# Split-operand query-key products in the stick-breaking group of a hybrid mixer trunk

## The chip, the cores and the metric

The kernel runs on one core of a Trainium2 chip. The metric is the device time of one execution in microseconds (us). The kernel before took 978.83 us, the median of three runs (978.14 to 978.84).

## The reference

One transformer block on x [512, 1024], fp32. Four mixers read the normed input: a causal pooling mixer, a dilated attention (12 heads of 64), a stick-breaking attention (4 heads of 128) and a diagonal state-space mixer (S5). Their outputs are gated, projected, summed and projected once more; then comes a gated feed-forward layer (FFN). The part that is changed is the first product of the stick-breaking group:

```python
xn = rmsnorm(x, attn_norm_g)
proj = xn @ w_in                      # 1024 -> 4864
y_sb = stick_breaking_attention(qkv_sb)
#   per block of 128 queries:
#   z = einsum('bhqe,bhke->bhqk', qb, kh) / sqrt(128)
#   w = where(mask, exp(log_sigmoid(z) + excl_cumsum(log_sigmoid(-z))), 0)
#   o = w @ vh
for yb, width in zip((y_pool, y_dil, y_sb, y_s5), BRANCH_WIDTHS):
    merged += sigmoid(xn @ w_gate[b]) * (yb @ w_branch[rows])
x = x + merged @ w_out                # "x2" in the kernel
x = x + (silu(hn @ w_up_g) * (hn @ w_up_u)) @ w_down   # hn = rmsnorm(x2)
```

## The kernel before

Every big product is done in three passes. A weight chunk is fetched by DMA (`raw`), ScalarE casts it to the rounded type fp32r (`hi`), VectorE subtracts (`lo = raw - hi`). The activations are split in the same way, and `mm3` adds hi·hi, hi·lo and lo·hi into one PSUM bank. `split(src, nm)` is the same for one 128x512 tile: a ScalarE copy into `<nm>h`, a VectorE subtraction into `<nm>l`, both in new slots. The few products that are left in plain fp32 go to TensorE as one instruction each; one of them shows in the profile as several records.

The order of the instructions on each engine is written by the Python program: the scheduler does not change it. The main stream goes through the weight chunks: the S5 input (u5), the dilated group's q, k and v (`qk`, `v`), then `sb_qk(0)`, `sb_v(0)`, `pool_u(0)`, `pool_u(1)`, `sb_qk(1)`, `sb_v(1)`, then the gates and branch projections of branch 0 (pool), 1 (dilated), 2 (stick-breaking), 3 (S5), the output projection `m_o`, and the FFN. Beside it run generators (`s5_gen`, `dil_gen`, `sb_gen`, `pool_gen`). The function `tick()`, called after most products of the main stream, lets each of them emit its next piece. It holds them back when the program's own count of time (`clock`, fed by the wrapper `_Paced`, which charges a plain fp32 product four times its columns) says that VectorE or ScalarE is more than MAX_LAG behind TensorE. So an edit of a cost or a count of instructions can move where later pieces stand in the queues. Every instruction that goes through `_Paced` is recorded with line 81, so instructions are told apart by the names of their tiles.

VectorE and ScalarE carry out their queues strictly in the written order: an instruction that waits holds up all behind it.

All 128x512 working tiles come out of one rotating pool, `slots`, of N_SLOTS buffers. When a new tile gets a buffer that another tile had, its first writer waits until the last reader of that other tile is done.

Names used below: `m_sqk` and `sqk` are a stick-breaking q or k product and its evacuation (`sb_qk`), `m_sv` the v product (`sb_v`), `s_z` the query-key product (`sb_gen`). `s_pw`, `yph`, `ypl` are the pooling mixer's group product and its split output; `p`, `ph`, `pl` its split input (`pool_gen`). `prob`, `s_pt`, `wt`, `s_po`, `ydil` are the dilated group's probabilities, their transposes on TensorE, these in SBUF, the product with v, and the sum. `pw_c`, `s_re`, `s_im`, `s_psy`, `h_re`, `h_im`, `ta`, `tb` belong to S5, where `s_psy` is a TensorE group that reads `pw_c` and `s_re`. `m_g` and `m_b` are the gate and branch products.

Of the kernel before, what the change touches and what calls it, by code (L numbers as in the profile page):

```python
# [43 lines left out]
CST_CNT = 512  # L44
CST_W = CST_CNT + 64

N_SLOTS = 61
N_RAW = 2
N_PM = 3
S5_RATE = 0.9  # L50
# [35 lines left out]
def _advance(clock, key, cost):  # L86
    clock[key] = cost + (clock[key] if key == "pe" else max(clock[key], clock["pe"]))
# [3 lines left out]
def hybrid_trunk(ctx: ExitStack, tc: tile.TileContext, a: dict, out: bass.AP):  # L91
# [5 lines left out]
    PE = _Paced(nc.tensor, lambda n: _advance(clock, "pe", max(0.42e-3 * n, 0.1)))  # L97
    ctx.enter_context(tc.manual_schedule())

    gp = ctx.enter_context(tc.tile_pool(name="consts", bufs=1))  # L100
    sp = ctx.enter_context(tc.tile_pool(name="slots", bufs=N_SLOTS))
    wp = ctx.enter_context(tc.tile_pool(name="weights", bufs=2))
# [10 lines left out]
    def nm_(nm):  # L113
        uid[0] += 1
        return f"{nm}_{uid[0]}"

    def slot(nm):
        return sp.tile([P, T], F32, tag="s", name=nm_(nm))
# [5 lines left out]
    def main_ps(nm):  # L124
        return pm.tile([P, T], F32, tag="mm", name=nm_("m_" + nm))

    def side_ps(nm):
        return pa.tile([P, T], F32, tag="at", name=nm_("s_" + nm))

    def r_(t):  # L130
        return t.bitcast(F32R)

    def split(src, nm, mk=None):
        mk = mk or slot
        hi = mk(nm + "h")
        lo = mk(nm + "l")
        A.copy(r_(hi), src)
        V.tensor_tensor(r_(lo), src, hi, ALU.subtract)
        return r_(hi), r_(lo)
# [124 lines left out]
    def next_chunk():  # L264
        c = used[0]
        used[0] += 1
        while len(loaded) < min(len(ready) + N_RAW, len(specs)):
            load_next()
        while len(ready) < min(c + 2, len(specs)):
            if specs[len(ready)][0] == "w_ups":  # L270
                flush(split_steps())
            else:
                split_next()
        return ready[c]

    def mm3(ps, ch, c, nw, acts, k0=0):
        n = len(acts)
        for k, (ah, al) in enumerate(acts):
            wh, wl = ch.h(k0 + k, c, P, nw), ch.l(k0 + k, c, P, nw)
            PE.matmul(ps, wh, ah, start=k == 0, stop=False)  # L280
            PE.matmul(ps, wh, al, start=False, stop=False)
            PE.matmul(ps, wl, ah, start=False, stop=k == n - 1)
# [8 lines left out]
    def tick(force=False):  # L291
        for e in list(active):
            e[3] += e[2]
            if e[3] < 1.0 and not force:
                continue
            e[3] -= 1.0
            if e[1] > 0:
                e[1] -= 1
                continue
            if max(clock["v"], clock["a"]) - clock["pe"] > MAX_LAG and not force:  # L300
                continue
            try:
                w = next(e[0])
                e[1] = (w or 1) - 1
            except StopIteration:
                active.remove(e)
# [10 lines left out]
    ps = side_ps("warm")  # L317
# [6 lines left out]
    for kt in range(KT):  # L324
        t = slot("x")
# [32 lines left out]
    def g2(kt):  # L358
        return cols[:, 8 + kt : 9 + kt]
# [5 lines left out]
    def sumsq_add(acc, src):  # L365
        sq = slot("sq")
        A.activation(sq, src, AF.Square)
        if acc is None:
            return sq
        V.tensor_tensor(acc, acc, sq, ALU.add)  # L370
        return acc
# [561 lines left out]
    sq, sk, sv = [], [], []  # L933
# [5 lines left out]
    def sb_gen():  # L939
        units = [(h, b) for h in range(4) for b in range(4)]  # L940
        bes, wts, pos = {}, {}, {}
        for s in range(len(units) + SB_T + SB_O):
            if s >= SB_T + SB_O:
                u = s - SB_T - SB_O
                h, b = units[u]
                if b == 0:
                    pos[h] = side_ps("sbo")
                for c in range(b + 1):
                    PE.matmul(
                        pos[h][:, b * P : (b + 1) * P],  # L950
                        sv[h // 2][c // 2][:, (c % 2) * 256 + (h % 2) * P : (c % 2) * 256 + (h % 2) * P + P],
                        wts[u][:, c * P : (c + 1) * P],
                        start=c == 0,
                        stop=c == b,
                    )
                if b == 3:
                    ysb.append(split(pos[h], "sb"))
            if SB_T <= s < len(units) + SB_T:
                u = s - SB_T
                h, b = units[u]  # L960
                n = (b + 1) * P
                pt = side_ps("wt")
                for c in range(b + 1):
                    PE.transpose(pt[:, c * P : (c + 1) * P], bes[u][:, c * P : (c + 1) * P], ident)
                wts[u] = slot("wt")
                A.copy(wts[u][:, :n], pt[:, :n])
            if s < len(units):
                h, b = units[s]
                n = (b + 1) * P
                dg = slice(b * P, n)  # L970
                ps = side_ps("z")
                PE.matmul(ps[:, :n], sq[h][:, dg], sk[h][:, :n], start=True, stop=True)
                be, om = slot("be"), slot("om")
                bes[s] = be
                A.activation(om[:, :n], ps[:, :n], AF.Sigmoid, scale=-z_scale)
                A.activation(be[:, :n], ps[:, :n], AF.Sigmoid, scale=z_scale)
                V.tensor_tensor(om[:, dg], om[:, dg], m_up, ALU.max)
                V.tensor_tensor(be[:, dg], be[:, dg], m_low, ALU.mult)
                V.tensor_tensor_scan(om[:, :n][:, ::-1], om[:, :n][:, ::-1], zcol.to_broadcast([P, n]), 1.0, ALU.mult, ALU.add)
                V.tensor_tensor(be[:, : n - 1], be[:, : n - 1], om[:, 1:n], ALU.mult)  # L980
            yield
# [88 lines left out]
    for g in range(3):  # L1070
        for lst, scale in ((dq, rb8), (dk, rb)):
            ch = next_chunk()
            for n in range(2):
                ps = main_ps("qk")
                mm3(ps, ch, n * P, 256, xg)
                t = slot("qk")
# [4 lines left out]
        if g == 0:  # L1081
            vt = [slot("v"), slot("v")]
            for b in range(4):
                ps = main_ps("v")
# [10 lines left out]
        else:  # L1095
            for n in range(2):
                ps = main_ps("v")
                mm3(ps, ch, n * P, 256, xg)
                t = slot("vf")
# [6 lines left out]
    def sb_qk(c):  # L1106
        for lst in (sq, sk):
            ch = next_chunk()
            for n in range(2):
                ps = main_ps("sqk")  # L1110
                mm3(ps, ch, n * P, 256, xg)
                t = slot("sqk")
                V.tensor_tensor(t, ps, rb, ALU.mult)
                lst.append(t)
                tick()

    def sb_v(c):
# [14 lines left out]
    def pool_u(c):  # L1132
        ch = next_chunk()
        for n in range(2):
# [5 lines left out]
            tick()  # L1140

    sb_qk(0)
    sb_v(0)
    pool_u(0)
    pool_u(1)
    sb_qk(1)
    sb_v(1)
    e_sb = start(sb_gen(), SB_RATE)


# [33 lines left out]
    for c in range(2):  # L1184
        ch = next_chunk()
        for n in range(2):
# [4 lines left out]
            t = slot("sg")  # L1191
# [4 lines left out]
    for kt in range(KT):  # L1196
        t = slot("xo")
# [8 lines left out]
    def keep(nm):  # L1206
        n = nm_(nm)
        return fp.tile([P, T], F32, tag=n, name=n)
# [3 lines left out]
    x2, x2g = [], []  # L1212
    acc = None
    for c in range(4):
        ch = next_chunk()
        for n in range(2):
            nt = 2 * c + n
            ps = main_ps("o")
            mm3(ps, ch, n * P, 256, mg)
            t = keep("x2")  # L1220
            V.tensor_tensor(t, ps, xo[nt], ALU.add)
            x2.append(t)
            hi, lo = slot("x2h"), slot("x2l")
            A.activation(r_(hi), t, AF.Copy, scale=g2(nt))
            V.scalar_tensor_tensor(r_(lo), t, g2(nt), hi, ALU.mult, ALU.subtract)
            x2g.append((r_(hi), r_(lo)))
            acc = sumsq_add(acc, t)
# [115 lines left out]
    for part in range(2):  # L1343
# [33 lines left out]
        for nt in range(8 - N_HALVED * part):  # L1377
# [8 lines left out]
            ps = main_ps("d")  # L1386
# [22 lines left out]
    def down_add(nt, hf, ps):  # L1409
        sl = slice(H * hf, H * hf + H)  # L1410
        V.tensor_tensor(x2[nt][:, sl], ps[:, 0:H], x2[nt][:, sl], ALU.add)
        sq = slot("sq")
        A.activation(sq[:, sl], x2[nt][:, sl], AF.Square)
        return sq
# [25 lines left out]
    for nt, ch in last:  # L1440
        ps = main_ps("d")
        down_half(nt, ch, 0, ps, kall)
        t = down_add(nt, 0, ps)
        V.tensor_tensor(acc[:, 0:H], acc[:, 0:H], t[:, 0:H], ALU.add)
    for nt, ch in last[:-1]:
        ps = main_ps("d")
        down_half(nt, ch, 1, ps, kall)
        t = down_add(nt, 1, ps)
# [5 lines left out]
    ps = main_ps("d")  # L1454
# [5 lines left out]
    t = down_add(nt, 1, ps)  # L1460
# [140 lines left out]
```

## Time and profile before

| | |
|---|---|
| median of 3 runs | 978.83 us (978.14 to 978.84) |
| the profiled execution | 980.17 us |
| its span | 978.4 us |
| TensorE busy | 963.7 us, 99% |
| VectorE busy | 656.8 us, 67% |
| ScalarE busy | 409.1 us, 42% |
| TensorE on the chain that ended last | 96% |

PE is TensorE, DVE is VectorE, ACT is ScalarE. Busy time is the time in which the engine had an instruction in work. The chain is followed back from the last instruction of the program: at each step to what released it, or to the instruction before it on the same engine. In the timelines, "[0.54 <-ACT hi L81]" behind an instruction says that its engine stood idle for 0.54 us before it, and what ended that. Matmuls overlap: one record of 0.39 us does not mean that the next started 0.39 us later, so costs are taken from the distance between starts.

### The profile page before, as it was taken

To read this page: it belongs to the slowest core of one execution; us is meant where nothing else is said; L and a number is where in the kernel's file an instruction comes from. 1 tells how busy PE (TensorE), PEld (TensorE's weight loads), DVE (VectorE), ACT (ScalarE), POOL (GpSimd) and SP (SyncE) were. 2 spreads that over 40 slices of the span, in tenths; PEclk is the share of its full clock that TensorE was granted. 3 is DMA by queue.
4 is the path that set the end of the run, shared out by engine and by line. 5 is a ranking of instruction groups with operands and counts; after the bars stand their busy time and mean duration, and the time that the engine had idled before them with its cause. 6 is when DMAs were issued, how large, how long until landed. Compare 5 with 4: busy or idle time off the path is not lost.

```text
span 978.4 us, 13757 instructions
## 1 busy us (share of the span) xinstructions
PE 963.7 (99%) x5426; PEld 831.3 (85%) x5426; DVE 656.8 (67%) x1253; ACT 409.1 (42%) x712; POOL 4.3 (0%) x20
## 2 busy tenths in 40 slices
PE   8999999999999999999999999999999999999996
PEld 6887888988888888887888888888898899999886
DVE  6576667588777976955645555488973379997344
ACT  7343533343446334227433343345442235554231
POOL 1000000000000000000000000000000000000000
PEclk9999999999999999999999999999999999999998
DMA  7442232231113113262342332313223323232212
GB/s 276 167 127 97 61 118 89 68 111 45 66 55 102 55 43 119 92 203 87 120 169 89 109 119 91 124 52 122 83 71 110 102 92 125 87 130 75 103 60 86
DMA packets 38696, 100.26 MB, mean 102 GB/s; under 512 B 14222, under 2 KB 22075, under 8 KB 32872
## 3 DMA queue, kind: packets, MB, share of 16 engines
q1 hardware_dynamic: 38632, 99.38, 30.2%
q8 instruction: 43, 0.70, 0.3%
q14 instruction: 21, 0.17, 0.1%
HBM read 94.94 MB, written 4.42 MB: 102 GB/s over the span
## 4 chain that ended last, share of the span: by engine, by line
PE 96%; DVE 2%; ACT 1%; DMA 1%; issue 0%; SPq 0%; DVEq 0%
PE m_g L81 17%; PE m_d L81 12%; PE s_fa L81 9%; PE m_b L81 7%; PE m_qk L81 7%; PE m_fb L81 6%; PE m_sqk L81 4%; PE m_o L81 4%; PE m_fg L81 4%; PE m_v L81 3%; PE m_u L81 3%; PE m_fu L81 3%; PE m_sv L81 2%; PE s_u L81 1%; PE s_fu L81 1%; PE m_gb L81 1%
## 5 line engine op out<-in xcount | busy, mean ns | idle before, releaser
L81 DVE TENSOR_TENSOR lo<-raw,hi 128x1024 fp32r<-128x1024 f32 (+5 forms) x207 | 197.8, 988 | 52.4 <-ACT hi L81 51.5
L81 ACT CAST hi<-raw 128x1024 fp32r<-128x1024 f32 (+5 forms) x207 | 169.3, 861 | 68.8 <-PE m_d L81 30.0
L81 PE MATMUL m_g<-xh,hi 128*128 128x512 f32 x256 | 102.7, 401 | 0.0
L81 PE MATMUL m_g<-xh,lo 128*128 128x512 f32 x256 | 100.0, 391 | 0.3 <-DVE lo L81 0.3
L81 PE MATMUL m_g<-xl,hi 128*128 128x512 f32 x256 | 99.7, 389 | 0.0
L81 PE MATMUL m_d<-hh,hi 128*128 128x512 f32 (+1 forms) x198 | 72.5, 366 | 0.0
L81 PE MATMUL m_d<-hl,hi 128*128 128x512 f32 (+1 forms) x198 | 72.4, 366 | 0.0
L81 PE MATMUL m_d<-hh,lo 128*128 128x512 f32 (+1 forms) x198 | 72.3, 365 | 0.0
L81 ACT ACTIVATE gt<-gt 128x512 f32<-128x512 f32 x32 | 20.2, 632 | 109.7 <-DVE gt L81 109.7
L81 PEld LDWEIGHTS m_g<-xh,lo 128*128 128x128 f32 x256 | 48.1, 188 | 11.2 <-DVE lo L81 1.0
L81 PEld LDWEIGHTS m_g<-xh,hi 128*128 128x128 f32 x256 | 48.1, 188 | 10.9 <-issue 1.0
L81 PEld LDWEIGHTS m_g<-xl,hi 128*128 128x128 f32 x256 | 48.1, 188 | 10.8 <-issue 1.0
L81 DVE TENSOR_TENSOR x<-m_d,x 128x512 f32<-128x512 f32 (+1 forms) x18 | 11.4, 632 | 62.6 <-PE m_d L81 62.6
L81 PEld LDWEIGHTS m_d<-hh,lo 128*128 128x128 f32 x198 | 37.3, 189 | 6.1
L81 PEld LDWEIGHTS m_d<-hh,hi 128*128 128x128 f32 x198 | 37.4, 189 | 6.0
L81 PEld LDWEIGHTS m_d<-hl,hi 128*128 128x128 f32 x198 | 37.4, 189 | 5.9
L81 DVE TENSOR_TENSOR gt<-m_b,gt 128x512 f32<-128x512 f32 x24 | 16.5, 689 | 38.0 <-PE m_b L81 32.8
L81 ACT ACTIVATE prob<-prob,nmx 128x128 f32<-128x128 f32 (+1 forms) x48 | 20.1, 419 | 49.3 <-DVE nmx L81 49.2
L81 DVE TENSOR_TENSOR raw<-raw 128x512 f32<-128x512 f32 (+1 forms) x45 | 39.1, 870 | 1.6
L81 PE MATMUL m_qk<-xh,hi 128*128 128x512 f32 x96 | 38.2, 397 | 0.0
L81 PE MATMUL m_qk<-xl,hi 128*128 128x512 f32 x96 | 37.4, 390 | 0.0
L81 PE MATMUL m_qk<-xh,lo 128*128 128x512 f32 x96 | 37.4, 390 | 0.0
(400 smaller groups left out, 2498.0 us busy)
## 6 DMA issues: line engine op xcount, KB each, us to landing
raw<-in_w_g SPq DMA_DIRECT2D x24, 768.0 KB, 4.3
raw<-in_w_in SPq DMA_DIRECT2D x17, 1024.0 KB, 6.9
raw<-in_w_ups SPq DMA_DIRECT2D x15, 1024.0 KB, 4.8
raw<-in_w_down SPq DMA_DIRECT2D x16, 704.0 KB, 4.0
raw<-in_w_up SPq DMA_DIRECT2D x7, 1024.0 KB, 4.8
raw<-in_w_g SPq DMA_DIRECT2D x8, 640.0 KB, 3.8
raw<-in_w_out SPq DMA_DIRECT2D x4, 1024.0 KB, 4.9
x<-in_x SPq DMA_DIRECT2D x8, 256.0 KB, 4.9
```

What stands on the lines that cost most here:

```text
L81: return f(out, *args, **kw)
```

## The change

The evacuated q and k tiles of the stick-breaking group are split into a rounded and a rest part. The query-key product becomes three fp32r passes on these parts where it was one plain fp32 product. The eight x2 tiles, which had buffers of their own in the FFN's pool, come from the rotating pool, and that pool has 67 buffers where it had 61.

```diff
-N_SLOTS = 61
+N_SLOTS = 67
...
-                PE.matmul(ps[:, :n], sq[h][:, dg], sk[h][:, :n], start=True, stop=True)
+                (qh, ql), (kh, kl) = sq[h], sk[h]
+                PE.matmul(ps[:, :n], qh[:, dg], kh[:, :n], start=True, stop=False)
+                PE.matmul(ps[:, :n], qh[:, dg], kl[:, :n], start=False, stop=False)
+                PE.matmul(ps[:, :n], ql[:, dg], kh[:, :n], start=False, stop=True)
...
                 V.tensor_tensor(t, ps, rb, ALU.mult)
-                lst.append(t)
+                lst.append(split(t, "sqk"))
...
-            t = keep("x2")
+            t = slot("x2")
```

There are 16 query-key products, four heads with 128, 256, 384 and 512 columns each, and eight q and k tiles, so eight new casts `sqkh` on ScalarE and eight new subtractions `sqkl` on VectorE. In the written order the change has effects in three places.

TensorE, the first query-key product, at the start of branch 0. The kernel before:

```order
L81 MATMUL s_po_2619<-wt_2471,v_654 64x128
L81 MATMUL s_po_2619<-wt_2559,v_654 64x128
L81 MATMUL s_pt_2636<-cst,prob_1254 128x128 [waits DVE_49] x4
L81 MATMUL s_z_2647<-sqk_1614,sqk_1519 128x128
L81 MATMUL m_b_2657<-yph_2176,hi_2383 128x512
L81 MATMUL m_b_2657<-ypl_2177,hi_2383 128x512
```

The changed kernel:

```order
L81 MATMUL s_pt_2623<-cst,prob_1019 128x128
L81 MATMUL s_z_2634<-sqkh_1624,sqkh_1521 128x128
L81 MATMUL s_z_2634<-sqkl_1625,sqkh_1521 128x128
L81 MATMUL s_z_2634<-sqkh_1624,sqkl_1522 128x128
L81 MATMUL m_b_2646<-yph_2100,hi_2383 128x512
L81 MATMUL m_b_2646<-ypl_2101,hi_2383 128x512
```

The place of the product in the stream is the same; three instructions stand where one stood, and other units of the dilated group are beside it.

VectorE, during `sb_qk(0)`, from the second q/k tile to the S5 operand `pw_c`. The kernel before:

```order
L81 TENSOR_SCALAR nmx<-stat_207 128x4
L81 TENSOR_TENSOR sqk_1558<-m_sqk_1533,rb 128x512
L81 TENSOR_TENSOR h_re_1354<-h_re_1354,sin_1073 128x512
L81 TENSOR_TENSOR h_im_1355<-h_im_1355,cos_1074 128x512
L81 TENSOR_TENSOR s_im<-h_re_1354,h_im_1355 128x4x127
L81 TENSOR_TENSOR lo_1584<-raw_1486,hi_1583 128x1024 x2
L81 TENSOR_TENSOR sqk_1614<-m_sqk_1589,rb 128x512
L81 TENSOR_TENSOR t_251_1616<-s5p,pwr_712 128x256
L81 TENSOR_TENSOR t_251_1616<-s5p,pwi_713 128x256
```

The changed kernel:

```order
L81 TENSOR_SCALAR nmx<-stat_207 128x4
L81 TENSOR_TENSOR sqk_1562<-m_sqk_1537,rb 128x512
L81 TENSOR_TENSOR sqkl_1565<-sqk_1562,sqkh_1564 128x512
L81 TENSOR_TENSOR h_re_1354<-h_re_1354,sin_1073 128x512
L81 TENSOR_TENSOR h_im_1355<-h_im_1355,cos_1074 128x512
L81 TENSOR_TENSOR s_im<-h_re_1354,h_im_1355 128x4x127
L81 TENSOR_TENSOR lo_1592<-raw_1486,hi_1591 128x1024 x2
L81 TENSOR_TENSOR sqk_1622<-m_sqk_1597,rb 128x512
L81 TENSOR_TENSOR sqkl_1625<-sqk_1622,sqkh_1624 128x512
L81 TENSOR_TENSOR t_257_1628<-s5p,pwr_712 128x256
L81 TENSOR_TENSOR t_257_1628<-s5p,pwi_713 128x256
```

Each subtraction stands directly behind the evacuation whose ScalarE copy it needs, and ahead of S5's instructions.

VectorE, at the end of `sb_qk(1)`, ahead of the v product `m_sv`; here with the engines that an instruction waits for. The kernel before:

```order
L81 TENSOR_TENSOR ydil_2159<-s_po_2304,ydil_2159 128x512 [waits PE_49]
L81 TENSOR_SCALAR prob_1366<-prob_1366,fp_1919 128x128 x4
L81 SCALAR_TENSOR_TENSOR ypl_2330<-s_pw_2325,cols,yph_2329 128x512 [waits Activation_49]
L81 TENSOR_TENSOR sqk_2358<-m_sqk_2333,rb 128x512 [waits PE_49]
L81 TENSOR_TENSOR h_re_2296<-h_re_2296,ta_2298 128x512 [waits DVE_49]
```

The changed kernel:

```order
L81 SCALAR_TENSOR_TENSOR ypl_2329<-s_pw_2324,cols,yph_2328 128x512 [waits PE_49,Activation_49]
L81 SCALAR_TENSOR_TENSOR p_2332<-s_356_2253,u_2077 128x496 [waits PE_49]
L81 TENSOR_TENSOR s_356_2253<-s_356_2253,cst 128x16
L81 TENSOR_TENSOR p_2332<-s_356_2253,u_2077 128x16 [waits DVE_49]
L81 TENSOR_TENSOR pl_2337<-p_2332,ph_2336 128x512 [waits PE_49,Activation_49]
L81 TENSOR_TENSOR sqk_2365<-m_sqk_2340,rb 128x512 [waits PE_49]
L81 TENSOR_TENSOR sqkl_2368<-sqk_2365,sqkh_2367 128x512 [waits Activation_49]
```

And on TensorE, what follows the first half of the v product in the changed kernel:

```order
L81 MATMUL m_sv_2417<-lo_2259,xh_174 128x256
L81 MATMUL s_po_2446<-wt_2236,v_1211 64x128 [waits PE_49]
L81 MATMUL s_po_2446<-wt_2318,v_1211 64x128 [waits Activation_49]
L81 MATMUL s_po_2446<-wt_2236,v_1211 64x128
```

One pooling unit (`p`, `pl`) has moved back behind `ypl`, and `ypl_2329` has a wait on TensorE that its counterpart `ypl_2330` did not have. The buffer that `ypl_2329` is given belonged to `wt_2236`, whose last readers are the `s_po_2446` products behind the 48 matmuls of `m_sv`.

## Rows read from the trace of the kernel before

**Rows 1.** The page, part 1: busy us, share, instructions, by engine.

```profile
PE 963.7 (99%) x5426; PEld 831.3 (85%) x5426; DVE 656.8 (67%) x1253; ACT 409.1 (42%) x712; POOL 4.3 (0%) x20
```

**Rows 2.** TensorE's waits: us in total, times, longest.

```profile
PE s_u L81 <- ACT hi L81: 2.9, 2, 1.5
```

**Rows 3.** TensorE's timeline in the FFN: start us, us, what, idle before.

```profile
697.87 0.39 PE L81 MATMUL s_fa<-xsh,hi 128*128 128x256 f32 x1 [1.62 <-ACT mu L81]
```

**Rows 4.** A window: us, busy (instructions) by engine, clock, DMA share, GB/s.

```profile
150.00:255.00 105.00, 105.00 (x660) 91.67 (x659) 78.46 (x188) 39.65 (x74) 0.00 (x0) 1.00 0.26 80
```

**Rows 5.** The chain, 165 to 290 us: start us, us, what.

```profile
173.03 11.51 PE m_sv L81 x96
...
239.12 0.44 PE s_pt L81 x4
...
262.90 0.22 PE s_z L81 x2
...
269.42 5.46 PE m_g L81 x24
...
276.60 0.65 PE s_z L81 x2
...
280.64 0.86 PE s_z L81 x2
```

**Rows 6.** VectorE's timeline in sb_qk(1), sb_v(1): start, us, what, idle before.

```profile
225.37 0.67 DVE L81 SCALAR_TENSOR_TENSOR p<-s,u 128x496 f32<-128x496 f32 x1
...
227.03 0.69 DVE L81 TENSOR_TENSOR pl<-p,ph 128x512 fp32r<-128x512 f32 x1 [0.69 <-ACT ph L81]
...
236.88 0.74 DVE L81 SCALAR_TENSOR_TENSOR ypl<-s_pw,cols,yph 128x512 fp32r<-128x512 f32 x1
...
239.76 0.68 DVE L81 TENSOR_TENSOR h_re<-h_re,ta 128x512 f32<-128x512 f32 x1
...
243.50 1.06 DVE L81 TENSOR_SCALAR prob<-prob,f 128x128 f32<-128x128 f32 x4
244.47 1.82 DVE L81 TENSOR_TENSOR lo<-raw,hi 128x768 fp32r<-128x768 f32 x2
...
248.14 0.68 DVE L81 TENSOR_TENSOR ydil<-s_po,ydil 128x512 f32<-128x512 f32 x1
```

**Rows 7.** VectorE's timeline in sb_qk(0).

```profile
154.50 0.68 DVE L81 TENSOR_TENSOR sqk<-m_sqk,rb 128x512 f32<-128x512 f32 x1
155.10 0.68 DVE L81 TENSOR_TENSOR ta<-h_re,cos 128x512 f32<-128x512 f32 x1
...
158.62 0.69 DVE L81 TENSOR_TENSOR sqk<-m_sqk,rb 128x512 f32<-128x512 f32 x1 [0.47 <-PE m_sqk L81]
...
161.77 2.36 DVE L81 TENSOR_TENSOR lo<-raw,hi 128x1024 fp32r<-128x1024 f32 x2 [0.54 <-ACT hi L81]
...
167.66 0.42 DVE L81 TENSOR_TENSOR pw_c<-t 64x256 f32<-64x256 f32 x1
```

**Rows 8.** ScalarE's timeline, same stretch.

```profile
158.19 0.40 ACT L81 ACTIVATE prob<-prob,nmx 128x128 f32<-128x128 f32 x1 [5.04 <-DVE nmx L81]
```

**Rows 9.** TensorE's timeline, same stretch.

```profile
170.41 0.39 PE L81 MATMUL s_psy<-s_re,pw_c 128*128 128x128 f32 x2
```

**Rows 10.** The chain of waits, 230 to 250 us.

```profile
232.97 0.70 PE s_pw L81 x3
...
239.55 5.74 PE m_sv L81 x48
245.29 1.02 PE s_po L81 x16
```

**Rows 11.** Windows as in rows 4, about three waits of TensorE.

```profile
8.00:12.00 4.00, 2.79 (x9) 1.94 (x9) 3.07 (x5) 3.87 (x6) 0.00 (x0) 0.84 1.06 405
12.00:16.00 4.00, 4.00 (x15) 3.19 (x14) 3.76 (x6) 3.94 (x7) 0.00 (x0) 0.73 1.11 387
...
698.00:702.00 4.00, 4.00 (x34) 4.00 (x35) 3.90 (x5) 1.89 (x4) 0.00 (x0) 1.00 0.73 262
```

## The prediction

> **What bounds the kernel now.** I read the engines' busy times first, then TensorE's waits, then one window around the change, then the chain and the timelines inside it. TensorE is busy for 963.7 of 978.4 us, VectorE for 67% and ScalarE for 42% [rows 1]. Its waits for other engines are few: the two largest entries are 2.9 us in two waits near the start [rows 2] and 1.62 us in one at 697.87 us, in the FFN [rows 3]. So nearly every microsecond of TensorE's queue counts, and the rest counts only where it makes TensorE wait. Between 150 and 255 us, where q, k, v and the pooling input of the changed group are made, TensorE does not idle at all, and VectorE works for 78.46 of 105 us [rows 4]: 75%, above its mean. All new VectorE work falls there. The question is whether the remaining 25% lies where it is wanted.
>
> **The query-key products.** On the chain the products of 128, 384 and 512 columns take 0.22, 0.65 and 0.86 us [rows 5]; in proportion the one of 256 takes 0.43. Four heads make 4 x 2.16 = 8.64 us. Each becomes three fp32r passes. The gate product has 24 such passes of 512 columns in 5.46 us, 0.2275 each; the v product has 96 of 256 columns in 11.51 us, 0.12 each [rows 5]. The line through both is 0.0125 us plus 0.42 ns a column, which gives 0.066 for 128 and 0.174 for 384 columns. After: 4 x 3 x (0.066 + 0.12 + 0.174 + 0.2275) = 7.05 us, a gain of 1.6. No row shows a 128-column pass in fp32r. At best the fixed part is nothing: the passes go by 0.42 ns a column, 1280 columns x 12 x 0.42 = 6.45 us, a gain of 2.2. At worst such a pass is as long as the whole plain product of that size, 0.22: then 12 passes take 2.64 instead of 0.79 and the edit costs 0.26. I take 1.6, by the line through the two nearest sizes; a plain 128-column transposition is 0.11 (four in 0.44 [rows 5]), and with that number the gain is 1.06.
>
> The passes of 256 columns, each with a load of other weights, follow one another after 0.12 us [rows 5]. The Trainium skill, "TensorE: Matmul & The Clock Gate", section "LDWEIGHTS (loading the stationary operand)", says that a load takes its columns divided by 1.2 in nanoseconds, 107 ns for 128. By that rule a 128-column pass would be bound by its load, at 0.107 instead of 0.066 us, and the sum would be higher by an estimated 0.5 us. No run here shows such a pass; 0.12 lies above both, so the row does not decide.
>
> **The splits in sb_qk(0).** A subtraction stands directly behind its evacuation, so VectorE waits for ScalarE's cast between the two. The nearest pair of that form is `ph` and `pl`: 0.69 us idle, then the subtraction [rows 6], which occupies 0.60 (the distance between the starts of neighbouring 512-column operations, 154.50 to 155.10 [rows 7]). So 1.3 to 1.4 us each; I use 1.37 with the hand-over. Eight make 11 us of VectorE's queue, and the price is what its idle time does not absorb. Behind the first (evacuated at 154.50) comes `nmx`, and the second evacuation had 0.47 us of idle ahead of it [rows 7]: it starts 0.9 late, at 159.5. Its cast is worse off, since it queues behind four exponentials on ScalarE, which began at 158.19 [rows 8] and now begin as late as `nmx` does; the subtraction cannot start before about 161.7, and S5's `h_re` behind it is 3.1 us late. The 0.54 of idle before `lo` [rows 7] gives back some: `lo` is 2.5 late, the next evacuation 1.7, and with its own subtraction `pw_c` is 3.06 late. The third `pw_c` ended at 168.08 (167.66 + 0.42 [rows 7]); its first reader, an `s_psy` product, started at 170.41 [rows 9]: 2.33 us of slack. So TensorE waits 0.7 us there. Bounds: nothing, if the casts slip in before the exponentials, and 2.2, if the second cast waits behind the two v copies as well.
>
> **The freed buffer in sb_qk(1).** Live at once are now eight more tiles (parts of q and k) with six more buffers, so buffers come round later. In the order, `ypl_2329` on VectorE waits for a TensorE reader of its buffer's last tenant, `wt_2236`; this reader stands behind the 48 matmuls of `m_sv`. Before, `ypl` ran at 236.88, ahead of `m_sv` at 239.55 [rows 6, 10]. VectorE's queue is strict, so from there to the end of the following `s_po` it does nothing. Call the start of `m_sv` A. `m_sv` takes 5.74 and `s_po` 1.02 [rows 10]: `ypl` starts at A+6.78. Queued behind it are a pooling unit's `p`, its cast and `pl`. `p` starts one `ypl` later, at A+7.43; from `p` to `pl` it took 1.66 (225.37 to 227.03 [rows 6]), so the cast ends and `pl` starts at A+9.09, and `pl` ends at A+9.78. TensorE goes on from `s_po` through `s_pt` (0.44 [rows 5]) and one `s_pw` group (0.70 [rows 10]) and stands at A+7.9 before the second `s_pw` group. Its first pass wants the cast and waits 1.2; the second pass, 0.23 later, wants `pl` and waits 0.5. Together **1.7 us**.
>
> TensorE then does the other half of `m_sv` and is at A+16.0 before `s_pt`, which reads a `prob` of VectorE's. VectorE, from A+9.78, has the fourth `sqk` of this stage with its split (0.60 + 0.69 + 0.60), `h_re` to the end of the scans (239.76 to 243.50, 3.74), `lo` to `ydil` (244.47 to 248.14, 3.67 [rows 6]), `ydil` itself (0.60) and the first `prob` (0.28): A+20.0. Before, `sqk` was already done when `m_sv` began, and none of this stood in arrears. So TensorE waits another **4.0 us**. Bounds of the two waits together: nothing, if VectorE gets to `ypl` only when the buffer is free anyway or the queue behind it has slack that I don't see; 7.5, if the casts on ScalarE are late by as much as in sb_qk(0). I take 5.7, as the chain of rows gives it. After these two VectorE has the room of branch 0 to catch up; the later query-key products keep their places.
>
> **The clock.** A wait of TensorE can cost more than itself. Near the start it waited 2.9 us [rows 2] and the granted clock was 0.84 from 8 to 12 and 0.73 from 12 to 16 us [rows 11]: taken as a mixture of the two levels, 1.2 and 2.4 GHz, this is 1.3 and 2.2 us at 1.2 GHz, which lost 1.7 us of work. Behind the single wait of 1.62 us at 697.87 it stayed at 1.00 [rows 3, 11]. A wait of 4.0 us that follows one of 1.7 by 6 us is more like the first. I charge one fall, 1.6 us; bounds: none, and two falls, 3.4.
>
> **The rest.** Eight more casts on ScalarE, 0.62 each, are hidden where they don't appear above: it is busy 42% of the time. x2 in the rotating pool moves nothing in the FFN's order; 67 - 8 = 59 buffers serve there where 61 did. The trace cannot show a reuse that gets tight; I price it at nothing, because every instruction keeps its place, and one wait, if it came, at about the 1.62 us of the one that the FFN has [rows 3].
>
> **The sum.** -1.6 + 0.7 + 1.7 + 4.0 + 1.6 = +6.4. The profiled execution took 980.17 us (span 978.4, and 1.8 around it), which makes 986.6; it was 1.3 over the median, 978.83, so the runs should give **985.2**.
>
> **Rivals.** *A: the splits are absorbed, the products alone count.* For it: VectorE has 25% free, and a TensorE wait on a buffer costs nothing if the buffer is free by then. Against it: the place of the reader, behind `m_sv`, while VectorE reached `ypl` 2.7 us before `m_sv` began. The point from which it decides is whether VectorE comes to `ypl` later than A+6.78. Then 978.83 - 1.6 = 977.2, or 976.6 with no fixed part: the other side, about at the limit of what can be told. *B: the waits come, the clock holds*, as at 697.87: 983.6. *C: one of the two waits in sb_qk(1) is absorbed*: 978.83 - 1.6 + 0.7 + 1.7 or 4.0, and no fall: 979.6 to 981.9. *D: the short passes are slow* (0.22 each, nothing else changed): 1.85 more, 987.1. *E: the clock falls more than once and the `s_psy` wait is 2.2*: 985.2 + 1.5 + 1.7 = 988.4.
>
> **Chances.** Forecast 0.38, B 0.26, A 0.14 (half of it below the limit), C 0.10, D 0.05, E 0.07. A measurement of this kernel can tell about 0.2% from no change: 976.87 to 980.79. Faster 0.07; the same 0.11 (the other half of A and not quite half of C); slower 0.82. The range 979.5 to 988.6 leaves out A and a little above; the forecast's own is 984 to 987.
>
> **What would show it.** The products: three `s_z` records where one set stood, 0.2, 0.36, 0.52 and 0.68 us on the chain. The splits: a wait of TensorE for VectorE before `s_psy` near 170 us. The buffer: VectorE idle for some 6 us before a `ypl`, released by `s_po`; then TensorE waiting for `ph`/`pl` before `s_pw`, and for `prob` before `s_pt`. The clock: a granted clock under 1 after that wait. It is wrong if no such idle time stands before `ypl`, if TensorE's waits grow elsewhere (in the FFN, at x2), or if `s_z` takes more than before.

## The result

The changed kernel takes 986.40 us (median of four runs, 986.08 to 988.25), the kernel before 978.84 on the same chip: a ratio of 1.0079, interval 1.0062 to 1.0097, or 7.6 us more. The forecast was 985.2.

The profile after, part 1 of its page: busy time, share of the span (984.2 us) and count of instructions.

```profile
PE 964.4 (98%) x5442; PEld 833.2 (85%) x5442; DVE 662.1 (67%) x1261; ACT 413.2 (42%) x720; POOL 4.3 (0%) x20
```

TensorE works as long as before [rows 1], and the span is 5.8 us longer. The sums over the whole program tell little; the list of TensorE's waits tells more (in total, times, longest):

```profile
PE s_pt L81 <- DVE prob L81: 3.5, 1, 3.5
PE s_u L81 <- ACT hi L81: 2.5, 2, 2.1
PE s_fa L81 <- ACT mu L81: 1.6, 1, 1.6
...
PE s_pw L81 <- ACT ph L81: 1.2, 1, 1.2
...
PE s_psy L81 <- DVE pw_c L81: 0.6, 1, 0.6
...
PE s_pw L81 <- DVE pl L81: 0.2, 1, 0.2
```

`s_u` and `s_fa` were there before [rows 2, 3]. The four others are new: `s_psy` in sb_qk(0), two before `s_pw` and one before `s_pt` around sb_v(1), 5.5 us together. The reason for the last three stands in VectorE's timeline there, which answers to [rows 6]:

```profile
237.23 0.87 DVE L81 TENSOR_SCALAR prob<-prob,fp 128x128 f32<-128x128 f32 x4
243.65 0.75 DVE L81 SCALAR_TENSOR_TENSOR ypl<-s_pw,cols,yph 128x512 fp32r<-128x512 f32 x1 [5.55 <-PE s_po L81]
244.32 0.67 DVE L81 SCALAR_TENSOR_TENSOR p<-s,u 128x496 f32<-128x496 f32 x1
...
246.02 0.69 DVE L81 TENSOR_TENSOR pl<-p,ph 128x512 fp32r<-128x512 f32 x1 [0.74 <-ACT ph L81]
246.63 0.68 DVE L81 TENSOR_TENSOR sqk<-m_sqk,rb 128x512 f32<-128x512 f32 x1
248.00 0.69 DVE L81 TENSOR_TENSOR sqkl<-sqk,sqkh 128x512 fp32r<-128x512 f32 x1 [0.69 <-ACT sqkh L81]
...
256.60 0.87 DVE L81 TENSOR_SCALAR prob<-prob,fp 128x128 f32<-128x128 f32 x4
```

VectorE stands idle for 5.55 us, released by `s_po`, before an instruction that ran without a wait before. From there to 256.60 its queue is one unbroken line of work but for two short casts, and at its end stands the `prob` that TensorE wants.

The pieces of the chain that answer to [rows 5] (start us, us, what):

```profile
169.48 2.84 PE s_psy L81 x22
...
256.93 1.10 PE s_pt L81 x4
258.03 6.70 PE m_g L81 x24
...
266.67 0.28 PE s_z L81 x3
266.95 2.82 PE m_b L81 x12
269.78 2.68 PE s_psy L81 x24
...
273.22 0.35 PE s_z L81 x3
273.57 5.45 PE m_g L81 x24
...
281.40 0.52 PE s_z L81 x3
...
285.33 0.70 PE s_z L81 x3
```

The products cost 0.28, 0.35, 0.52 and 0.70 us, 7.4 for all, where they cost 8.64. A little of that comes back in the twelve branch passes directly behind a product of 128 columns. Before, the first such group was shorter:

```profile
263.12 2.75 PE m_b L81 x12
```

In all four heads the branch passes at this place take 2.82, 2.82, 2.78 and 2.78 us in the changed kernel, 11.20 together, where they took 11.01; the gain is 1.2 on the products alone and 1.0 with these.

The first 24 gate passes after the long wait take 6.70 us, the next 24 take 5.45. The clock accounts for it, in windows as in [rows 11] (clock: the eighth column, behind POOL's busy time):

```profile
8.00:12.00 4.00, 2.87 (x11) 2.06 (x12) 3.15 (x5) 3.94 (x7) 0.00 (x0) 1.00 1.04 392
12.00:16.00 4.00, 4.00 (x20) 3.28 (x19) 3.68 (x6) 3.97 (x7) 0.00 (x0) 1.00 1.06 380
254.00:258.00 4.00, 1.07 (x5) 0.99 (x6) 3.97 (x10) 0.84 (x2) 0.00 (x0) 0.89 0.61 197
258.00:262.00 4.00, 4.00 (x14) 3.15 (x13) 3.96 (x10) 3.33 (x4) 0.00 (x0) 0.69 0.00 0
```

After the wait of 3.55 us part of the time runs at 1.2 GHz. At the start it is the other way round: this execution has 1.00 there where the profiled one of before had 0.84 and 0.73, which lost it 1.7 us. So 5.8 + 1.7 = 7.5 us are to be explained between the two traces, which agrees with the 7.6 of the medians.

### The profile page after: what moved, and what is told of

Same layout as the page of the kernel before. It is cut to its first block, busy times and chain, and to the rows that moved or that the text cites. A ratio compares the mean times of both kernels' runs of the same rounds, so it can differ in the third digit from the quotient of the medians.

```text
span 984.2 us, 13807 instructions
## 1 busy us (share of the span) xinstructions
PE 964.4 (98%) x5442; PEld 833.2 (85%) x5442; DVE 662.1 (67%) x1261; ACT 413.2 (42%) x720; POOL 4.3 (0%) x20
## 4 chain that ended last, share of the span: by engine, by line
PE 91%; DVE 5%; ACT 2%; issue 1%; DMA 1%; SPq 0%; DVEq 0%; ACTq 0%
PE m_g L81 17%; PE m_d L81 12%; PE s_fa L81 9%; PE m_b L81 7%; PE m_qk L81 7%; PE m_fb L81 6%; PE m_o L81 4%; PE m_fg L81 4%; PE m_u L81 3%; PE m_fu L81 3%; PE m_v L81 2%; PE m_sqk L81 2%; PE m_sv L81 2%; DVE lo L81 1%; PE s_fu L81 1%; PE m_gb L81 1%
```

## The experiments

**One buffer more.** 68 buffers instead of 67.

```diff
-N_SLOTS = 67
+N_SLOTS = 68
```

> The changed kernel with 68 buffers in place of 67. In VectorE's queue this frees only the one ypl of its wait for TensorE; the p directly behind it still gets a buffer whose last reader stands behind m_sv. Theory (VectorE's strict queue is held by a buffer that TensorE frees only after m_sv): VectorE still idles, now before p; the first wait (s_pw for ph) shrinks by one ypl, 0.65 us, the later one of 3.5 us for prob stays: about 985.7, 0.7 less than the changed kernel. Rival 1 (the pool is short by a single buffer): both waits go and the time is about 979. Rival 2 (the waits come from the added work on VectorE, buffers don't matter): 986.4, no change.

Measured: 985.69 us, 1.0068 of the kernel before (1.0056 to 1.0081). TensorE's waits, and VectorE's timeline at the place:

```profile
PE s_pt L81 <- DVE prob L81: 3.6, 1, 3.6
...
PE s_pw L81 <- ACT ph L81: 0.5, 1, 0.5
```

```profile
239.87 0.75 DVE L81 SCALAR_TENSOR_TENSOR ypl<-s_pw,cols,yph 128x512 fp32r<-128x512 f32 x1
...
245.46 0.68 DVE L81 SCALAR_TENSOR_TENSOR p<-s,u 128x496 f32<-128x496 f32 x1 [4.84 <-PE s_po L81]
```

`ypl` runs at once, and the next instruction takes its place as the one that is held: 4.84 us of idle in place of 5.55, the same releaser. The first wait shrank by 0.7 us, the later one stayed, as the theory had it. The time alone does not decide: the loss is 6.2 us over the kernel before timed beside it (979.54), where it was 7.6, and the two intervals overlap. The rows decide against rivals 1 and 2. A window behind the waits shows the clock, the figure behind POOL's:

```profile
255.00:300.00 45.00, 41.91 (x275) 35.13 (x276) 36.43 (x89) 19.09 (x41) 0.00 (x0) 0.96 0.21 65
```

**The low parts unread.** The same instructions on VectorE and ScalarE in the same order up to branch 0, but eight tiles come free at once.

```diff
-                PE.matmul(ps[:, :n], qh[:, dg], kh[:, :n], start=True, stop=False)
-                PE.matmul(ps[:, :n], qh[:, dg], kl[:, :n], start=False, stop=False)
-                PE.matmul(ps[:, :n], ql[:, dg], kh[:, :n], start=False, stop=True)
+                PE.matmul(ps[:, :n], qh.bitcast(F32)[:, dg], kh.bitcast(F32)[:, :n], start=True, stop=True)
```

> The changed kernel, but the query-key product is one plain fp32 product of the two rounded parts; the rest parts are computed and never read, so the products lack their low bits. VectorE and ScalarE do the same instructions in the same order up to branch 0; what differs is that the eight unread rest parts give their buffers back at once, and ypl and p lose their wait for TensorE. Theory (buffers): no wait of TensorE near 245 to 257 us, the one of 0.6 before s_psy stays with some 0.4 of restart; the products cost 8.64 as before: about 979.8. Rival (the added VectorE and ScalarE work itself makes the waits): 986.4 + 1.2 for the plain products = 987.6.

Measured: 980.78 us against 979.54 of the kernel before timed beside it, 1.0017 (1.0008 to 1.0027). VectorE's timeline:

```profile
239.70 0.86 DVE L81 TENSOR_SCALAR prob<-prob,fp 128x128 f32<-128x128 f32 x4
240.48 0.74 DVE L81 SCALAR_TENSOR_TENSOR ypl<-s_pw,cols,yph 128x512 fp32r<-128x512 f32 x1
241.14 0.66 DVE L81 SCALAR_TENSOR_TENSOR p<-s,u 128x496 f32<-128x496 f32 x1
...
253.42 0.86 DVE L81 TENSOR_SCALAR prob<-prob,fp 128x128 f32<-128x128 f32 x4
```

VectorE no longer idles before `ypl`, and the second group of `prob` starts 13.7 us after the first (253.42 - 239.70), where it takes 19.4 in the changed kernel (256.60 - 237.23). Among TensorE's waits past the start and ahead of the FFN one of some size is left:

```profile
PE s_psy L81 <- DVE pw_c L81: 0.5, 1, 0.5
```

This is the run that shows the cause: all of the added VectorE and ScalarE work is still there, and the loss falls from 7.6 us to 1.2, although the products are back at their old price. What made the three waits was how long eight tiles hold their buffers.

**x2 alone.** The kernel before with the second part of the change.

```diff
-N_SLOTS = 61
+N_SLOTS = 67
...
-            t = keep("x2")
+            t = slot("x2")
```

> The kernel before with only the second part of the change: x2 in the rotating pool and 67 buffers. The order on every engine is that of before. Theory: 978.8, the same within 0.5. Rival (x2's place costs a wait in the FFN, or more buffers help the kernel before): more than 1 us to either side.

Measured: 980.15 us against 979.54, 1.0006 (0.9998 to 1.0015): not to be told from no change. Its list of waits has the entries of before and no other.

**The subtraction after tick().** With 68 buffers.

```diff
-                lst.append(split(t, "sqk"))
-                tick()
+                hi, lo = slot("sqkh"), slot("sqkl")
+                A.copy(r_(hi), t)
+                tick()
+                V.tensor_tensor(r_(lo), t, hi, ALU.subtract)
+                lst.append((r_(hi), r_(lo)))
```

> The changed kernel with 68 buffers, and the subtraction of each q and k split emitted after tick() in place of directly behind the evacuation, so that other VectorE work stands between it and ScalarE's cast. This also moves the dilated and pooling units back to earlier ticks, and the ypl ahead of m_sv has no wait for TensorE. Theory: all three waits go and the products' gain of 1.2 is left: about 977.6. Rival (the added work makes the waits wherever it stands): 983 or more.

> The same kernel as subtract_after_tick, on the chip of this group, as the base of the five-fold products and to see its sign: 1.0 below the kernel before by its trace from the first v product to the end of the query-key products, 0.2 below by its first timing.

Measured: 979.29 us against 979.54, 0.9995 (0.9986 to 1.0004), and again 978.30 against 978.95, 0.9995 (0.9987 to 1.0004). The window of [rows 4], in the first of the two:

```profile
150.00:255.00 105.00, 105.00 (x658) 91.49 (x657) 80.46 (x189) 43.41 (x82) 0.00 (x0) 1.00 0.26 80
```

TensorE does not idle, and VectorE works for 80.46 us in it, more than before. So the added work does fit, at this order and with 68 buffers. The time is not above that of the kernel before, but the gain of 1.2 that was expected isn't shown either: the two medians lie 0.25 and 0.65 us lower, inside their intervals. It is the best version found, and no faster than the kernel before as far as can be told.

**Only the last subtraction late.** 67 buffers; the edit of the run above for the last q/k tile only.

```diff
+                if c == 1 and lst is sk and n >= 1:
...
+                else:
                     lst.append(split(t, "sqk"))
                     tick()
```

> The changed kernel with 67 buffers; only the last of the eight subtractions is emitted after tick(), the others stay directly behind their evacuations. The ypl keeps its buffer wait behind m_sv, but the VectorE queue behind it is shorter by one wait for ScalarE, and units of the dilated and pooling groups move. Theory (the chain of VectorE work behind the held ypl sets the later wait): TensorE's wait for prob falls from 3.5 to about 1.4 us. If the clock holds behind such a wait, as behind the 1.62 us in the FFN, the time is 978.8 - 1.2 + 1.0 (s_psy) + 1.4 + 0.3 (restart) + 0.7 (a new wait of the stick-breaking transposes for ScalarE) = 981.0; if it falls as behind the 3.5 us, 982.9. Rival (the last subtraction isn't on the path): 986.4.

Measured: 981.43 us, 1.0029 (1.0018 to 1.0040). TensorE's wait and the window behind it:

```profile
PE s_pt L81 <- DVE prob L81: 1.3, 1, 1.3
```

```profile
250.00:254.00 4.00, 4.00 (x36) 4.00 (x35) 3.97 (x8) 1.18 (x4) 0.00 (x0) 1.00 0.23 43
```

The time and the wait came close to what the theory gave, but two premises of the expectation were wrong. The new wait of 0.7 us of the stick-breaking transposes, a term of its 981.0, does not stand in TensorE's list of waits, so the sum was met in part by luck. And it said that `ypl` keeps its buffer wait; VectorE's timeline shows none:

```profile
238.73 0.87 DVE L81 TENSOR_SCALAR prob<-prob,fp 128x128 f32<-128x128 f32 x4
239.50 0.75 DVE L81 SCALAR_TENSOR_TENSOR ypl<-s_pw,cols,yph 128x512 fp32r<-128x512 f32 x1
...
247.40 0.87 DVE L81 TENSOR_SCALAR prob<-prob,fp 128x128 f32<-128x128 f32 x4
```

The one late subtraction also gave the tiles other buffers. The wait of 1.3 us comes from the length of VectorE's queue at another order of units, so this run does not bear on the held buffer. It does bear on the clock: behind 1.33 us of waiting it stays at 1.00.

**The products five times.** Each product is repeated, and the last one counts; in the kernel before (shown) and, with all three passes repeated, in the one with the subtraction after tick().

```diff
+                for _ in range(4):
+                    nc.tensor.matmul(ps[:, :n], sq[h][:, dg], sk[h][:, :n], start=True, stop=True)
                 PE.matmul(ps[:, :n], sq[h][:, dg], sk[h][:, :n], start=True, stop=True)
```

> The kernel before with every query-key product done five times (the last one counts), to price it by the clock on the wall. If TensorE's queue is the bound there, four more times 8.64 us come on top: +34.6, about 1013.7. Rival (part of the product lies beside a wait of TensorE): less, down to +30.

> The kernel with the subtraction after tick() and 68 buffers, every query-key product (three passes) done five times. By the line through the passes of 256 and 512 columns (7.05 us for all): +28.2 over it, 1007.4. By the chain of the changed kernel (0.28, 0.355, 0.525, 0.70; 7.44 for all): +29.8, 1009.0. With 0.11 for each pass of 128 columns, as the plain transposition of that size: +30.3. The difference to the five-fold product of the kernel before, divided by four, is the gain of the product: 1.6, 1.2 or 1.1.

Measured: 1014.04 us, 1.0360 of the kernel before (1.0346 to 1.0374), 35.1 us over its base (978.95) for four times 8.64 = 34.6; and 1009.35, 1.0313 (1.0299 to 1.0327), 31.1 us over its base (978.30). So the products are on the path in full in both, and the gain is (35.1 - 31.1) / 4 = 1.0 us for the 16 of them. Each sum is known to some 1.4 us, so the gain is known to about 0.5: it speaks for 1.2 or 1.1 rather than 1.6, weakly. The passes themselves show it better, TensorE's timeline of the second of these kernels:

```profile
262.46 0.28 PE L976 MATMUL s_z<-sqkh,sqkl 128*128 128x128 f32 x1
262.57 0.28 PE L974 MATMUL s_z<-sqkh,sqkh 128*128 128x128 f32 x1
262.68 0.27 PE L975 MATMUL s_z<-sqkl,sqkh 128*128 128x128 f32 x1
262.79 0.28 PE L976 MATMUL s_z<-sqkh,sqkl 128*128 128x128 f32 x1
```

Passes of 128 columns follow each other after 0.11 us. The line through 256 and 512 columns gave 0.066.

## Why the prediction was right

Step by step, forecast and trace:

| term | forecast, us | measured, us |
|---|---|---|
| query-key products | -1.6 | -1.0 |
| wait before `s_psy` | 0.7 | 0.56 |
| waits before `s_pw` | 1.7 | 1.21 + 0.22 |
| wait before `s_pt` | 4.0 | 3.55 |
| the clock behind it | 1.6 | 1.9 |
| getting going again after waits | not in the sum | about 1.1 |
| sum | 6.4 | 7.5, of 7.5 |

The clock's 1.9 is 6.70 - 5.45 for the gate passes and 1.10 - 0.44 for the four `s_pt` that opened them. By the granted clock of the two windows, 0.89 and 0.69, it would be 4 x (0.11 + 0.31) = 1.7, so a little of it may belong to the row below.

The total of the forecast was closer than its terms. The three waits were put 0.9 us too long together; the clock was put 0.3 too short, the products 0.6 too good, and the 1.1 of getting going again was left out. That the first of these errors made up for half of the others was luck. The mechanism was not: each wait came where the forecast had it, for the reason that it gave.

*The splits in sb_qk(0).* VectorE did wait for each cast, and the second was the bad one, as reckoned:

```profile
154.22 0.69 DVE L81 TENSOR_TENSOR sqkl<-sqk,sqkh 128x512 fp32r<-128x512 f32 x1 [0.69 <-ACT sqkh L81]
...
160.12 0.69 DVE L81 TENSOR_TENSOR sqkl<-sqk,sqkh 128x512 fp32r<-128x512 f32 x1 [1.64 <-ACT sqkh L81]
...
169.01 0.42 DVE L81 TENSOR_TENSOR pw_c<-t 64x256 f32<-64x256 f32 x1
```

The second cast came right behind the four exponentials, ahead of the v copies, and VectorE idled for 1.64 us where the reckoning has 1.6. At this point the execution is 1.65 us ahead of the one of before, for what happened at the start; so 169.01 answers to 170.66 there, and `pw_c` is 3.0 us later than the 167.66 of [rows 7], where 3.06 was reckoned. The wait remained in the run with the low parts unread (0.5), where buffers played no part: it is the price of a subtraction placed directly behind its cast, and it went when the subtraction stood after tick().

*The freed buffer.* This was the main term, and the one with a rival on the other side (A, that the waits are absorbed and only the products count). Its deciding point was whether VectorE comes to `ypl` later than the buffer is free; it came 5.55 us early. The run with the low parts unread removes the buffer waits and keeps the order of VectorE and ScalarE, and most of the loss goes with them. One buffer more does not, since `p` behind it needed one as well. C, that one of the two waits goes, was wrong: both came, and E's second fall of the clock did not.

*The clock.* One fall was charged and one came, behind the 3.55 us. With one buffer more the earlier waits were 0.5 and 0.2 instead of 1.2 and 0.2, and the mean clock from 255 to 300 us was 0.96 in both; the shorter waits ahead made no difference that can be seen. B, that the clock holds, was wrong here, and right where the wait was 1.33. But the comparison that the fall was charged by is weak. The kernel with x2 alone has the two waits near the start that the kernel before has (2.9 us together, the longer one 1.5), and in the windows of its trace the clock does not fall behind them, where that of before went to 0.84 and 0.73 [rows 11]:

```profile
8.00:12.00 4.00, 2.39 (x9) 1.69 (x10) 2.74 (x5) 3.48 (x6) 0.00 (x0) 1.00 1.06 403
12.00:16.00 4.00, 4.00 (x20) 3.30 (x19) 3.81 (x7) 3.93 (x7) 0.00 (x0) 1.00 1.09 380
```

So the length of such waits does not settle whether the clock falls, and what does stays open. Behind the wait of 3.55 us, and the 3.6 of the run with one more buffer, it fell; that one fall was charged was a guess that came out.

*The products.* The term that was mis-sized. The forecast took 0.066 us for a pass of 128 columns, from a line; it is 0.11. Twelve such passes are 0.55 us, so the line's 1.6 becomes 1.05. The trace has 1.0, with the branch passes directly behind the products counted in, and so have the five-fold products. The Trainium skill's rule in "TensorE: Matmul & The Clock Gate", section "LDWEIGHTS (loading the stationary operand)", 107 ns for a load of 128 columns, gave 1.1: the spacing in the trace agrees with it (0.11), though no run shows that the load is what sets it. I had the row against which to weigh the line (0.11 for a plain transposition of that size [rows 5]) and went by the line. D, 0.22 for such a pass, was wrong.

*What the sum left out.* After a wait TensorE does not continue at its pace at once. In the changed kernel 22 `s_psy` records behind the wait take 2.84 us, and 24 undisturbed ones 2.68, so the wait of 0.56 cost about 0.4 more. The three `s_pw` passes behind the other wait stand so in TensorE's timeline:

```profile
244.43 0.40 PE L81 MATMUL s_pw<-ph,pwl 128*128 128x512 f32 x1
246.04 0.50 PE L81 MATMUL s_pw<-ph,pwh 128*128 128x512 f32 x1 [1.21 <-ACT ph L81]
246.76 0.50 PE L81 MATMUL s_pw<-pl,pwh 128*128 128x512 f32 x1 [0.22 <-DVE pl L81]
247.10 0.40 PE L81 MATMUL s_pw<-ph,pwl 128*128 128x512 f32 x1
247.37 0.38 PE L81 MATMUL m_sv<-hi,xh 128*128 128x256 f32 x1
247.59 0.28 PE L81 MATMUL m_sv<-hi,xl 128*128 128x256 f32 x1
```

From the last pass ahead of the wait (244.43) to the second pass of `m_sv` (247.59) it is 3.16 us. Undisturbed, these are four passes of `s_pw` and one of `m_sv`, about 0.93 + 0.12 = 1.05 by [rows 10]. The difference is 2.11, and the waits in it are 1.43: another 0.7.

## What to carry to other kernels

Where tiles come from one rotating pool, the price of an edit that keeps more tiles alive need not be their work. Here it was the instruction that is given a buffer whose last reader stands far behind in another engine's queue, and everything behind that instruction in the engine's queue waited too. Look for it in the written order, as a new wait on an engine that the instruction did not use to wait for, and work out the lateness of the whole queue behind it, not the one instruction's. A short pass on TensorE is not priced by a line through long ones.

## What the runs showed of the hardware that I had not expected

The spacing of fp32r passes hardly falls from 256 columns to 128: it is 0.23 us at 512 columns, 0.17 at 384, 0.12 at 256, but still 0.11 at 128. So three such passes save 0.16 us over a plain fp32 product of 512 columns (0.86 to 0.70), and at 128 columns they cost 0.28 against 0.22, and some 0.05 more in the passes behind.

Part of the scatter of this kernel's times sits at its start: there the clock was 1.00 throughout in one profiled execution and down to 0.73 in the other, 1.7 us with no difference in that part of the program. A third, with x2 alone, had the waits of the slower of these two and the clock of the faster.

At two places waits cost TensorE more than their length while the clock stayed at 1.00: 0.4 us on top of 0.56, and 0.7 on top of 1.43.
